# A hybrid attention and SSD layer on one core: where its last projection's weights are loaded and summed, and how far ahead its tiles are fetched

## The chip, the cores and the metric

One core of a Trainium2 chip runs the whole kernel in one launch. The metric is the device time of that launch in microseconds (us), the median of several runs. TensorE (PE) multiplies; VectorE (DVE), ScalarE (ACT) and GpSimd (POOL) do elementwise work; SyncE (SP) only issues transfers. ACT can issue transfers too.

## What is computed

One layer over 1024 positions of width 1024, in float32. The reference, cut to what matters here:

```python
h = rmsnorm(x, pre_norm_mix) * (1.0 + scale_m) + shift_m
q_lat, kv_lat, k_idx, w_idx, z, xbc, dt_raw, g_a, g_b = split(h @ w_in)
y_a = sparse_mla_attention(...) @ w_o_attn
y_b = ssd_mixer(z, xbc, dt_raw, ...) @ w_o_ssd      # begins with a causal convolution of xbc
mix = (sigmoid(g_a) * y_a + sigmoid(g_b) * y_b) @ w_out
x = x + gate_m * rmsnorm(mix, post_norm_mix)
h2 = rmsnorm(x, pre_norm_ffn) * (1.0 + scale_f) + shift_f
u_gate, u_up = split(h2 @ w_ffn_in)                 # 1024 -> 2 x 2816
f = (silu(u_gate) * u_up) @ w_ffn_out               # 2816 -> 1024
x = x + gate_f * rmsnorm(f, post_norm_ffn)
```

## The kernel before

Activations lie transposed: 128 channels on the partitions, 512 positions (one *half*, `b` = 0 or 1) along the free dimension. Every float32 factor is split into a rounded part `hi` and a remainder `lo`, and a product is three matmuls, hi by hi, lo by hi and hi by lo. A weight piece of 128 x 512 is loaded by SP, its `hi` is made by ACT and its `lo` by POOL; an activation's `lo` is mostly made by DVE. So a weight passes through three engines before PE can use it, and its raw buffer is free again when POOL is done.

Instructions are traced in program order. A scheduler (`TC = dict(schedule_with_timeline_sim=True)`) then gives each engine an order of its own; buffers are handed out from rotating sets (`bufs=`), and semaphores follow from the data. An engine works strictly in the order it was given, and SP's queue likewise: an instruction that waits holds up all behind it. The kernel steers this order with edges that cost no semaphore: `in_order` fixes PE's order to the program's, and `behind` puts an instruction after the one that `barrier` holds for its engine. A `Stream` (`W`) loads the weights of most stages (`load`, lines L144 to L153); `next` keeps two pieces ahead of the one in use.

The stages, in the order in which PE works through them:

- Projections. `FILL` gives 44 weight tiles: five groups of four convolution tiles (`conv_group`, `conv`), 16 z tiles, 8 gate tiles. The first are worked on beside the indexer, from 79 us on.
- Attention with its `beside` work: `ada_slow` (L310 on) forms columns of the modulation by 64 multiplications on POOL from buffers tagged `adaw` (two of them). Then the SSD scan.
- `merge(b)` (L1241 on): for each of eight tiles, 48 matmuls `pos` with `w_o_ssd`; then the gates `d_gb`, `d_sga` and the attention output `d_ya` are loaded and combined with the result (L1249 to L1258), and the merged tile is split.
- `mixed(b)`, the matmuls `pot` with `w_out`, then `residual_steps`: row sums, `rstd` (PE, then DVE, then the power `r` on POOL, L265), `rspread` (PE, `prn`, L271), the residual sum, and the same once more for the next norm. `ffn_input` (L1326 on) applies the modulation; for half 0 it makes `h2h` and `h2l`.
- The FFN's first projection uses seven products in place of eight (a Strassen scheme over two halves of channels, positions and inputs). `ffn_sums` makes the sums of activations that it needs. `early` computes two of the products for 18 tiles and fills PE beside half 1's residual: `for n in (2, 1, 9, 2)` says how many of its steps stand before each step of the residual. It writes its results to DRAM, except for the last two tiles, which it keeps (`KEPT`, `held`). `gate_up(t)` does the other five products of a tile, of 12 matmuls each: it loads four weight quarters (`a11`, `a12` from the upper rows, `a21`, `a22` from the lower; tags `w0` with four buffers, `w1` with three), makes sums of them on DVE (L1447, L1448, L1462, L1465; `s1`, `s2` in tag `w2`, three buffers), splits each (`w_parts`, L1389 on ACT, L1390 on POOL), and evicts with DVE (L1454, L1461, L1464, L1467).
- Between the `gate_up` tiles stand 12 `weight_sums` units (L1496 on). Each loads four pieces of `w_ffn_out`, makes four differences of them on POOL (L1502 to L1505), and stores them to `d_t` in DRAM.
- The output projection, seven products again (0 to 6), each with four column tiles `c`, and 33 matmuls for each. `ffn_w` (L1589 on) loads a weight piece through SP from `w_ffn_out` or `d_t` (L1593) and splits it; the split pieces rotate through five `hi` and five `lo` buffers. `prepare` makes the next product's activations during this one's tiles: it loads `al` tiles from `d_a` (L1545; tag EV, nine buffers for everything), sums them on DVE into `S2` and `S3` (L1559 to L1562), and splits. ACT or DVE evicts each column tile. At the end come the last row sums and the output.

Of the kernel before, what the change touches and what calls it, by code (L numbers as in the profile page):

```python
# [67 lines left out]
def build(tc, a, dbg=None, stop=99, slots=None):  # L68
# [56 lines left out]
    def behind(ins):  # L125

        i = ins.ins
        if i.engine in barrier:
            tc.add_manual_dep(i, barrier[i.engine], mybir.DependencyInfo(
                mybir.DependencyClass.NoSync, mybir.DependencyReason.DATA), reason="behind")  # L130


    class Stream:
# [13 lines left out]
        def load(self):  # L147
            src, kt = self.q[len(self.tiles)]
            raw, hi, lo = self.tile(0, F32), self.tile(1, F32R), self.tile(2, F32R)
            behind(SP.dma_start(raw[:, :kt], src))  # L150
            behind(S.activation(hi[:, :kt], raw[:, :kt], AF.Copy))  # L151
            behind(G.tensor_tensor(lo[:, :kt], raw[:, :kt], f(hi[:, :kt]), op=OP.subtract))  # L152
            self.tiles.append((hi, lo))  # L153
# [157 lines left out]
    def ada_slow(j):  # L311
# [3 lines left out]
        for h, t in enumerate(ts):  # L315
            behind(SP.dma_start(t, a["ada_w"][j - 16][:, 4 * h:4 * h + 4]))
            behind(G.tensor_tensor(t, t, cs[:, 4 * h:4 * h + 4, None].to_broadcast([P, 4, P]), op=OP.mult))  # L317
# [617 lines left out]

    def conv_group(g):
        for t in group_tiles(g):
            conv_out(conv(*t))

# [300 lines left out]

    def merge(b, alloc):  # L1241

        MG = []
        for t in range(8):
            W.plan(col_tile(a["w_o_ssd"][t]))
            p = bank_d("pos")
            dense([(p, b, ALL)], wpieces(list(range(16))), YB[b])
            m, ld = EV("mrg"), EV("sgb")
            SP.dma_start(ld, d_gb[t][:, half(b)])  # L1249
            S.activation(ld, ld, AF.Sigmoid)  # L1250
            V.tensor_tensor(m, p, rys[b], op=OP.mult)
            G.tensor_tensor(m, m, ld, op=OP.mult)
            ld, ga = EV("yal"), EV("sgal")
            SP.dma_start(ld, d_ya[t][:, half(b)])
            SP.dma_start(ga, d_sga[t][:, half(b)])
            S.activation(ga, ga, AF.Sigmoid)
            V.tensor_tensor(ld, ld, ga, op=OP.mult)
            V.tensor_tensor(m, m, ld, op=OP.add)  # L1258
            hi, lo = alloc("mg")
            split_to(m, hi, lo)  # L1260
            MG.append(([hi] * 2, [lo] * 2))
        return MG
# [63 lines left out]
    def ffn_input(b, x1):  # L1326

        for t in range(8):
            h2 = x1[t]
            if b == 0:  # L1330
                hi, lo = H_("h2h", dt=F32R), H_("h2l", dt=F32R)
                S.activation(hi, h2, AF.Identity, bias=mod[:, 24 + t:25 + t], scale=am2[:, t:t + 1])
            V.tensor_scalar(h2, h2, am2[:, t:t + 1], mod[:, 24 + t:25 + t], op0=OP.mult, op1=OP.add)
# [47 lines left out]
    def w_load(part, name, t, h):  # L1381
        r = w_tile(part, name)
        i = SP.dma_start(r, a["w_ffn_in"][t][:, 4 * h:4 * h + 4]).ins
        barrier[i.engine] = i.name
        return r
# [23 lines left out]
    held = {}  # L1409

    def early(ts):

        for t in ts:
            w = [w_parts(w_load(0, "a1", t, h)) for h in BS]
# [12 lines left out]
            else:  # L1427
                held[t] = p1, g
            yield

    def gate_up(t):

        a11, a12 = w_load(0, "a11", t, 0), w_load(0, "a12", t, 1)
        a21, a22 = w_load(1, "a21", FT + t, 0), w_load(1, "a22", FT + t, 1)
        if t in held:
            p, (p1, g0) = bank("p0"), held[t]
# [9 lines left out]
        s1, s2 = w_tile(2, "s1"), w_tile(2, "s2")  # L1446
# [32 lines left out]
    with in_order(mybir.EngineType.PE):  # L1479
# [3 lines left out]
        for n in (2, 1, 9, 2):  # L1483
# [7 lines left out]
    KH = FT // 2  # L1491
    KP = (0, 4, 8)
    d_t = dr.tile([4, 4, P, KH, P], F32, name="d_t")
    ws4 = con.tile([P, 4, 4, P], F32, name="ws4", tag="mk")

    def weight_sums(c, k0):  # L1496

        n = min(4, KH - k0)
        b11, b12, b21, b22 = (ws4[:, i, 0:n] for i in range(4))
        for x, t, o in ((b11, c, 0), (b12, 4 + c, 0), (b22, 4 + c, KH), (b21, c, KH)):  # L1500
            behind(SP.dma_start(x, a["w_ffn_out"][t][:, o + k0:o + k0 + n]))
        G.tensor_tensor(b11, b12, b11, op=OP.subtract)  # L1502
        G.tensor_tensor(b12, b22, b12, op=OP.subtract)
        G.tensor_tensor(b22, b22, b11, op=OP.subtract)
        G.tensor_tensor(b21, b22, b21, op=OP.subtract)  # L1505
        for i, x in enumerate((b11, b22, b12, b21)):
            SP.dma_start(d_t[i, c][:, k0:k0 + n], x)

    units = [(c, k0) for c in range(4) for k0 in KP]
# [26 lines left out]
    xs = [[] for _ in range(7)]  # L1536

    def parts(i, src):
        xs[i].append(pair())
        split_to(src, *xs[i][-1])  # L1540

    def raw_a(k, b):

        t = EV("al")
        SP.dma_start(t, d_a[k][:, half(b)])  # L1545
        return t

    def a11(k):
        parts(0, raw_a(k, 0))

    def a12(k):
        parts(1, raw_a(KH + k, 0))

    def a22(k):
        parts(2, raw_a(KH + k, 1))

    def sums(k):
        x21, x22, x11 = raw_a(k, 1), raw_a(KH + k, 1), raw_a(k, 0)
        V.tensor_tensor(S2[k], x21, x22, op=OP.add)  # L1559
# [3 lines left out]

    def sum2(k):
        parts(3, S2[k])

    def sum3(k):
        if k < len(S3):
            x = S3[k]
        else:  # L1570
            x, x21 = raw_a(k, 0), raw_a(k, 1)
            V.tensor_tensor(x, x, x21, op=OP.subtract)
        parts(4, x)

    def sum1(k):
        x = raw_a(k, 0)
        V.tensor_tensor(x, x, S2[k], op=OP.add)
        parts(5, x)

    def sum4(k):  # L1580
        x = raw_a(KH + k, 0)
        V.tensor_tensor(x, x, S2[k], op=OP.subtract)
        parts(6, x)
# [5 lines left out]
    def ffn_w(src, k0, where=None):  # L1589
# [3 lines left out]
        ld = SP.dma_start(raw, src[:, k0:k0 + n]).ins  # L1593
        barrier[ld.engine] = ld.name
# [19 lines left out]
    def squared(src, sacc):  # L1614

        sq = EV("sqm")[:, 0:src.shape[1]]
        S.activation(sq, src, AF.Square)
        if sacc is not None:
            V.tensor_tensor(sq, sq, sacc, op=OP.add)
        return sq  # L1620

    def x1_load(b):

        for t in range(8):
            behind(SP.dma_start(x1s[b][t], d_x1[t][:, half(b)]))
# [10 lines left out]
    wo = a["w_ffn_out"]  # L1636
    sacc = [None, None]
    with in_order(mybir.EngineType.PE):
        for k in range(KH):
            a11(k)  # L1640
        def each(fn, ks=range(KH)):
            return [(fn, k) for k in ks]

        def mixed_up(x, y):
            return [i for two in zip_longest(x, y) for i in two if i]

        ahead = [mixed_up(each(a12), each(sums, range(3))), mixed_up(each(a22), each(sums, range(3, 9))),
                 each(sums, range(9, KH)) + each(sum2), each(sum3), each(sum1), each(sum4), []]

        def prepare(i, c):  # L1650
            todo = ahead[i]
            for fn, k in todo[len(todo) * c // 4:len(todo) * (c + 1) // 4]:
                fn(k)

        srcs = ([wo[c] for c in range(4)], [wo[c][:, KH:FT] for c in range(4)], [d_t[3, c] for c in range(4)],
                [d_t[1, c] for c in range(4)], [d_t[2, c] for c in range(4)], [d_t[0, c] for c in range(4)],
                [wo[4 + c][:, KH:FT] for c in range(4)])

        def product(i, p, c, start):
            prepare(i, c)  # L1660
            for _ in whole(p, [ffn_w(srcs[i][c], k0) for k0 in KP], xs[i], ALL, start):
                pass

        def banks(alloc):
            return [(bank_d if i < alloc else bank)("pfo") for i in range(4)]

        X = banks(0)
        for c in range(4):
            product(0, X[c], c, True)
            S.activation(p1s[c], X[c], AF.Copy)  # L1670
        for c in range(4):
            product(1, X[c], c, False)
            S.activation(fv[0][c], X[c], AF.Copy)
            sacc[0] = squared(X[c], sacc[0])
        X = banks(3)
        for c in range(4):
            product(2, X[c], c, True)
            S.activation(p4s[c], X[c], AF.Copy)
        X = banks(0)
        for c in range(4):  # L1680
            product(3, X[c], c, True)
            V.tensor_tensor(u2s[c], X[c], p1s[c], op=OP.add)
        for c in range(4):
            product(4, X[c], c, False)
            V.tensor_tensor(u3s[c], X[c], p1s[c], op=OP.add)
            V.tensor_tensor(p4s[c], u3s[c], p4s[c], op=OP.subtract)
            sacc[1] = squared(p4s[c], sacc[1])
        X = banks(3)
        for c in range(4):
            product(5, X[c], c, True)  # L1690
            V.tensor_tensor(p1s[c], X[c], u3s[c], op=OP.add)
            sacc[1] = squared(p1s[c], sacc[1])
        x1_load(1)
        for c in range(2):
            product(6, X[c], c, False)
            V.tensor_tensor(u2s[c], X[c], u2s[c], op=OP.add)
# [3 lines left out]
            else:  # L1700
                outputs(1, 0, 512, r, False, False)
        ws = [[ffn_w(srcs[6][c], k0, pair()) for k0 in KP] for c in (2, 3)]
        x1_load(0)
        sums_of = {}
        for sl in (slice(0, 256), slice(256, 512)):
            sq = sacc[0][:, sl]
            for c in (2, 3):
                p = X[c][:, sl]
# [85 lines left out]
```

## Time and profile before

| | |
|---|---|
| median of 3 runs | 2418.3 us (2414.1 to 2419.4) |
| the profiled execution | 2417.7 us, of which its span 2415.9 |
| PE at work | 2334.8 us, 97% of the span |
| DVE / ACT / POOL at work | 1530.8 / 1234.6 / 1164.9 us |
| moved by DMA | 385.05 MB, mean 159 GB/s |
| transfers issued from ACT's queue | 720 packets of 237315 |

The columns of the windows view are: the window and its length in us, then for PE, PEld (weight loads), DVE, ACT and POOL the busy time with the count of instructions, then the granted TensorE clock as a share of full speed, the busy share of the DMA engines and GB/s. In the waits view a row says who waited, on which line, for whom: the sum in us, the number of waits, the longest. In a timeline a row has its start, its duration, the engine (a q stands for its queue of transfers), line, operation, output and inputs, and in brackets the idle time before it and what ended that. In a view of one tile's instructions three durations are the least, the median and the most, in ns.

### The profile page before, as it was taken

How to read it: one execution, taken by the hardware profiler on the slowest of the kernel's cores; microseconds unless marked ns; L12 is line 12 of the kernel's file. 1: busy time of each engine (PE TensorE's matmuls, PEld its weight loads, DVE VectorE, ACT ScalarE, POOL GpSimd, SP SyncE). 2: the span in 40 equal slices, each digit the busy share in tenths (PEclk: the TensorE clock that was granted, in tenths of full speed). 3: DMA queues.
4: the chain of work that ended last, by engine and by line, in shares of the span. 5: the costliest groups of instructions: out<-in, count | busy, mean ns of one | idle time of the engine just before them, and what ended most of it. 6: DMA issues, size and time to landing. Idle time of an engine off the chain costs nothing.

```text
span 2415.9 us, 34903 instructions
## 1 busy us (share of the span) xinstructions
PE 2334.8 (97%) x11808; PEld 1914.8 (79%) x11808; DVE 1530.8 (63%) x2961; ACT 1234.6 (51%) x2376; POOL 1164.9 (48%) x915
## 2 busy tenths in 40 slices
PE   7999999999999999999999999999999999999997
PEld 5788888888887888887877877878777887888786
DVE  4566776499656666666678774445376665638565
ACT  4446665567445555556676654534454222345432
POOL 2721112322234455443445546556577677765645
PEclk9999999999999999999999999999999999999998
DMA  7223212522212222324678775654464676558455
GB/s 273 92 88 128 70 62 79 165 93 92 101 57 92 98 97 79 103 96 138 224 246 277 227 249 198 217 181 165 159 220 138 210 248 237 190 182 307 149 178 170
DMA packets 237315, 385.05 MB, mean 159 GB/s; under 512 B 23968, under 2 KB 91728, under 8 KB 237136
## 3 DMA queue, kind: packets, MB, share of 16 engines
q1 hardware_dynamic: 236416, 382.24, 47.5%
q8 instruction: 93, 1.52, 0.3%
q14 instruction: 86, 0.70, 0.1%
q10 hardware_dynamic: 720, 0.58, 0.1%
HBM read 288.07 MB, written 97.80 MB: 160 GB/s over the span
## 4 chain that ended last, share of the span: by engine, by line
PE 47%; DVE 7%; POOL 5%; DMA 5%; issue 4%; ACT 3%; SPq 1%; POOLq 0%; DVEq 0%; ACTq 0%
PE p L1396 9%; PE pw L236 7%; PE pos L226 6%; PE pfo L1610 4%; PE plg L780 4%; PE pot L226 3%; PE po L829 2%; PE pt L813 2%; PE poa L236 2%; POOL wr L1390 2%; PE puq L226 2%; DMA ws<-w_ffn_out 1%; DMA al<-d_a 1%; PE pyd L1077 1%; PE pst L1082 1%
## 5 line engine op out<-in xcount | busy, mean ns | idle before, releaser
L152 POOL TENSOR_TENSOR wlo<-wraw,whi 128x512 fp32r<-128x512 f32 x246 | 344.2, 1402 | 524.3 <-ACT whi L151 461.9
L1396 PE MATMUL p<-xh,wr 128*128 128x512 f32 x880 | 276.1, 392 | 9.4 <-DVE u L1461 5.1
L151 ACT ACTIVATE whi<-wraw 128x512 fp32r<-128x512 f32 x246 | 153.5, 626 | 196.6 <-issue 45.2
L1396 PEld LDWEIGHTS p<-xh,wr 128*128 128x128 f32 x880 | 166.5, 189 | 46.7 <-DVE u L1461 6.0
L1390 POOL TENSOR_TENSOR wr<-a,wr 128x512 fp32r<-128x512 f32 x110 | 153.9, 1413 | 55.9 <-ACT wr L1389 47.7
L1396 PE MATMUL p<-xl,wr 128*128 128x512 f32 x440 | 172.2, 391 | 0.0
L247 POOL TENSOR_TENSOR fwl<-fw,fwh 128x512 fp32r<-128x512 f32 (+1 forms) x78 | 112.0, 1441 | 107.1 <-ACT fwh L246 100.8
L792 ACT ACTIVATE lg<-lg,mx 128x256 f32<-128x256 f32 (+7 forms) x128 | 99.0, 773 | 71.0 <-DVE mx L789 70.0
L317 POOL TENSOR_TENSOR adaw<-adaw,cs 128x512 f32<-128x512 f32 x64 | 66.7, 1043 | 128.2 <-DMA adaw<-ada_w 113.4
L1389 ACT ACTIVATE wr<-a 128x512 fp32r<-128x512 f32 x110 | 68.0, 628 | 114.3 <-PE p L1396 92.1
L1396 PE MATMUL p<-h2h,wr 128*128 128x512 f32 x352 | 111.7, 394 | 0.0
L640 ACT ACTIVATE junk<-acc,cand__2203 128x1024 bf16<-128x1024 f32 (+2 forms) x96 | 86.2, 898 | 45.8 <-DVE cand__2203 L683 29.9
L226 PE MATMUL pos<-yh,wlo 128*128 128x512 f32 x256 | 101.0, 395 | 3.9 <-POOL wlo L152 3.8
L591 DVE SCALAR_TENSOR_TENSOR acc<-rel,widx,acc 128x384 f32<-128x384 f32 (+2 forms) x90 | 87.1, 987 | 24.9 <-ACT rel L586 24.7
L586 ACT ACTIVATE rel<-prel 128x512 f32<-128x512 f32 (+3 forms) x160 | 77.1, 523 | 48.6 <-PE prel L585 45.0
L226 PE MATMUL pos<-yh,whi 128*128 128x512 f32 x256 | 100.8, 394 | 0.3 <-ACT whi L151 0.3
L226 PE MATMUL pos<-yw,whi 128*128 128x512 f32 x256 | 100.4, 392 | 0.0
L1396 PEld LDWEIGHTS p<-xl,wr 128*128 128x128 f32 x440 | 83.2, 189 | 17.2
L638 DVE TENSOR_SCALAR_CACHE_REDUCE junk<-acc,cand__2212 128x896 bf16<-128x896 f32 (+2 forms) x96 | 88.5, 922 | 1.5
L813 PE MATMUL pt<-ident,lg 128*128 128x128 f32 x576 | 84.2, 275 | 5.0 <-ACT lg L792 4.5
L789 DVE CUSTOM_DVE_ANT_0 lg<-plg,nm 128x256 f32<-128x256 f32 (+1 forms) x128 | 51.5, 403 | 58.4 <-PE plg L780 57.7
L818 ACT ACTIVATE pc<-pt 128x512 f32<-128x512 f32 (+1 forms) x104 | 58.1, 562 | 52.6 <-PE pt L813 51.4
(657 smaller groups left out, 7286.9 us busy)
## 6 DMA issues: line engine op xcount, KB each, us to landing
wraw<-w_in SPq DMA_DIRECT2D x129, 256.0 KB, 2.7
a<-w_ffn_in SPq DMA_DIRECT2D x124, 256.0 KB, 3.3
al<-d_a SPq DMA_DIRECT2D x92, 256.0 KB, 4.7
adaw<-ada_w SPq DMA_DIRECT2D x64, 256.0 KB, 2.9
al<-d_ac SPq DMA_DIRECT2D x32, 512.0 KB, 5.9
wraw<-w_o_ssd SPq DMA_DIRECT2D x64, 256.0 KB, 3.4
d_a<-g SPq DMA_DIRECT2D x40, 256.0 KB, 3.1
ada<-ada_p SPq DMA_DIRECT2D x16, 512.0 KB, 6.2
```

Source lines behind the costliest of these rows:

```text
L151: behind(S.activation(hi[:, :kt], raw[:, :kt], AF.Copy))
L152: behind(G.tensor_tensor(lo[:, :kt], raw[:, :kt], f(hi[:, :kt]), op=OP.subtract))
L226: T.matmul(o, wt[:, k0 + i, :], xs[k][xi][b][:, sl], start=pi == 0 and i == 0 and wt is hi and xi == 0, stop=pi == len(pcs) - 1 and i == l ...
L236: T.matmul(o, wt[:, k0 + j, :], xs[k][xi][b], start=i == 0, stop=i == 23)
L247: (lo_eng or V).tensor_tensor(lo, src, f(hi), op=OP.subtract)
L638: V.tensor_scalar(jk, y, a_, 0.0, op0=op, op1=OP.add, accum_out=o)
L780: T.matmul(p[:, 0:w2], st[qi], KVT[ki][:, o_:o_ + w2], start=x == 0, stop=x == 2)
L792: S.activation(lg[:, 0:n], lg[:, 0:n], AF.Exp, scale=-1.0, bias=m, accum_out=rr[:, 2 * t + hh:2 * t + hh + 1])
L813: T.transpose(ptv[:, hh, t, :], PR[hh, t][:, j * P:(j + 1) * P], ident)
L1390: G.tensor_tensor(w[:, 1], src, f(w[:, 0]), op=OP.subtract)
L1396: T.matmul(p, w[:, wi, i], X[x][i][xi], start=start and i == 0 and k == 0, stop=i == 3 and k == 2, skip_group_check=True)
L1610: T.matmul(p, w[wi][:, k - k0], xs[k][xi][:, sl], start=start and k == 0 and i == 0, stop=k == KH - 1 and i == 2, skip_group_check=True)
```

## The change

1. **Weight sums.** The 12 `weight_sums` units move from between the `gate_up` tiles to behind the last 12 convolution tiles (groups 2 to 4). Their buffers are now the two `adaw` tiles and the two halves of attention's `vt` tile; their loads stand behind the last weight load issued on SP. `ada_slow`'s loads move behind the weight load that is current at the fourth z tile.
2. **Merge.** The three loads and both sigmoids, and the product of two of them, stand before the tile's matmuls. `ffn_input`'s instructions on ACT and DVE go behind the last merged tile's split, and `barrier` on SP becomes the last of the merge's loads.
3. **`early` and `gate_up`.** The lower weights of the two kept tiles are loaded during `early`, and their upper weights are kept (one pair in the `vt` tile). Lower weights rotate through five buffers (`w1` and `adaw`), the sums through five (`w2`, `uh`, `ul`). The list becomes (2, 1, 9, 3). These loads no longer move `barrier`.
4. **Output projection.** Weight pieces are loaded by ACT's queue (`S.dma_start`). Activations are loaded one step (one column tile) before the step that works on them. Some of the sums move: 0 and 1 into product 0, four of them share the loads of product 1, the rest stand in product 2. The first instruction of most preparations is chained behind the last eviction on its engine (`mark`, `held_to`). `x1_load(0)` moves ahead of the last weights.

The diff, cut to its core:

```diff
     def conv_group(g):
         for t in group_tiles(g):
             conv_out(conv(*t))
+            if g > 1:
+                weight_sums(*next(units))
...
         elif kind == "z":
             t = next(n_z)
             gate(1 + t, d_z[t], AF.Silu)
+            if t == 3:
+                ada_after = [W.issue]
...
         for t in range(8):
             W.plan(col_tile(a["w_o_ssd"][t]))
+            sb, ld, ga = EV("sgb"), EV("yal"), EV("sgal")
+            for x, src in ((sb, d_gb), (ld, d_ya), (ga, d_sga)):
+                i0 = SP.dma_start(x, src[t][:, half(b)]).ins
+            S.activation(sb, sb, AF.Sigmoid)
+            S.activation(ga, ga, AF.Sigmoid)
+            V.tensor_tensor(ld, ld, ga, op=OP.mult)
             p = bank_d("pos")
             dense([(p, b, ALL)], wpieces(list(range(16))), YB[b])
...
+    LOWER = [("w1", n_slots["hi"])] * 3 + [("adaw", 2)] * 2
+    SUMS = [("w2", n_slots["lo"])] * 3 + [("uh", 1), ("ul", 1)]
...
+            if t == EARLY - KEPT - 1:
+                low_w = [lower(EARLY - KEPT + i) for i in range(KEPT)]
...
-        for n in (2, 1, 9, 2):
+        for n in (2, 1, 9, 3):
...
-    for n, t in enumerate([*range(EARLY - KEPT, EARLY), *range(EARLY - KEPT), *range(EARLY, FT)]):
+    for t in [*range(EARLY - KEPT, EARLY), *range(EARLY - KEPT), *range(EARLY, FT)]:
         gate_up(t)
-        for u in units[12 * max(0, n - 4) // 18:12 * max(0, n - 3) // 18]:
-            weight_sums(*u)
...
         raw = w_tile(0, "fw")[:, 0:n]
-        ld = SP.dma_start(raw, src[:, k0:k0 + n]).ins
-        barrier[ld.engine] = ld.name
+        S.dma_start(raw, src[:, k0:k0 + n])
...
+    def held_to(ins):
+        i = ins.ins
+        if i.engine in last:
+            tc.add_manual_dep(i, last[i.engine], mybir.DependencyInfo(
+                mybir.DependencyClass.NoSync, mybir.DependencyReason.DATA), reason="behind")
...
+        def step(i, c):
+
+            n = 4 * i + c
+            loaded.append([load() for load, _ in tasks[n + 1]])
+            for (_, work), x in zip(tasks[n], loaded[n]):
+                work(x)
+            return [ffn_w(srcs[i][c], k0) for k0 in KP] if n < 26 else None
```

More of the change, by code (lines that the diff above doesn't have):

```diff
@@ L149, in load @@
             raw, hi, lo = self.tile(0, F32), self.tile(1, F32R), self.tile(2, F32R)
-            behind(SP.dma_start(raw[:, :kt], src))
+            self.issue = behind(SP.dma_start(raw[:, :kt], src))
             behind(S.activation(hi[:, :kt], raw[:, :kt], AF.Copy))
@@ L934, in group_tiles, with weight_sums @@
         return (16 + g, d_bc[g, 0]), (24 + g, d_bc[g, 1]), (2 * g, d_xs[2 * g]), (2 * g + 1, d_xs[2 * g + 1])
+    KH = FT // 2
+    d_t = dr.tile([4, 4, P, KH, P], F32, name="d_t")
+    units = iter([(c, k0) for c in range(4) for k0 in (0, 4, 8)])
+    sum_bufs = [wp.tile([P, 4, P], F32, name="adaw", tag="adaw", bufs=2) for _ in range(2)]
+    both = vp.tile([P, NT, P], F32, name="vt", bufs=1)
+    sum_bufs += [both[:, 0:4], both[:, 4:8]]
+    def weight_sums(c, k0):
+        n = min(4, KH - k0)
+        b11, b12, b21, b22 = (x[:, 0:n] for x in sum_bufs)
+        for x, t, o in ((b11, c, 0), (b12, 4 + c, 0), (b22, 4 + c, KH), (b21, c, KH)):
+            tc.add_manual_dep(SP.dma_start(x, a["w_ffn_out"][t][:, o + k0:o + k0 + n]).ins, W.issue, mybir.DependencyInfo(
+                mybir.DependencyClass.NoSync, mybir.DependencyReason.DATA), reason="behind")
+        G.tensor_tensor(b11, b12, b11, op=OP.subtract)
+        G.tensor_tensor(b12, b22, b12, op=OP.subtract)
+        G.tensor_tensor(b22, b22, b11, op=OP.subtract)
+        G.tensor_tensor(b21, b22, b21, op=OP.subtract)
+        for i, x in enumerate((b11, b22, b12, b21)):
+            SP.dma_start(d_t[i, c][:, k0:k0 + n], x)
     def conv_group(g):
@@ L1536, in build, with mark, raw_a, parts @@
     xs = [[] for _ in range(7)]
[L1538 to L1559, printed above, removed]
+    last = {}
+    def mark(ins):
+        last[ins.ins.engine] = ins.ins.name
+    def held_to(ins):
+        i = ins.ins
+        if i.engine in last:
+            tc.add_manual_dep(i, last[i.engine], mybir.DependencyInfo(
+                mybir.DependencyClass.NoSync, mybir.DependencyReason.DATA), reason="behind")
+    def raw_a(*which):
+        ts = [EV("al") for _ in which]
+        for t, (k, b) in zip(ts, which):
+            SP.dma_start(t, d_a[k][:, half(b)])
+        return ts
+    def parts(i, src, anchored=False):
+        hi, lo = pair()
+        xs[i].append((hi, lo))
+        ins = S.activation(hi, src, AF.Copy)
+        if anchored:
+            held_to(ins)
+        V.tensor_tensor(lo, src, f(hi), op=OP.subtract)
+    def plain(i, k0, b):
+        return [(lambda k=k: raw_a((k0 + k, b)), lambda x: parts(i, x[0], True)) for k in range(KH)]
+    def sum_of(k, x21, x22, x11):
+        held_to(V.tensor_tensor(S2[k], x21, x22, op=OP.add))
         V.tensor_tensor(S2[k], S2[k], x11, op=OP.subtract)
@@ L1624, in x1_load @@
         for t in range(8):
-            behind(SP.dma_start(x1s[b][t], d_x1[t][:, half(b)]))
+            SP.dma_start(x1s[b][t], d_x1[t][:, half(b)])
     def outputs(b, c0, cn, r, share, end):
@@ L1636, in build @@
     wo = a["w_ffn_out"]
+    low, high = [wo[c] for c in range(4)], [wo[c][:, KH:FT] for c in range(8)]
     sacc = [None, None]
     with in_order(mybir.EngineType.PE):
[L1639 to L1662, printed above, removed]
@@ L1679, in build @@
[L1679 to L1685, printed above, removed]
+        for k in ks:
+            parts(0, raw_a((k, 0))[0])
+        loaded = [[load() for load, _ in tasks[0]]]
+        srcs = low, high[0:4], d_t[3], d_t[1], d_t[2], d_t[0], high[4:8]
+        def step(i, c):
[4 more added lines that the diff above has]
+            return [ffn_w(srcs[i][c], k0) for k0 in KP] if n < 26 else None
@@ new lines, in products, with four @@
+        def products(i, alloc=None):
+            for c in range(4):
+                ws = step(i, c)
+                for _ in whole(banks[c], ws, xs[i], ALL, alloc is not None):
+                    pass
+                yield c, banks[c]
+        def four(alloc):
+            return [(bank_d if i < alloc else bank)("pfo") for i in range(4)]
+        banks = four(0)
+        for c, p in products(0, 0):
+            mark(S.activation(p1s[c], p, AF.Copy))
+        for c, p in products(1):
+            S.activation(fv[0][c], p, AF.Copy)
+            sacc[0] = squared(p, sacc[0])
@@ L1686, in build @@
+        banks = four(3)
+        for c, p in products(2, 3):
+            mark(S.activation(p4s[c], p, AF.Copy))
+        banks = four(0)
+        for c, p in products(3, 0):
+            mark(V.tensor_tensor(u2s[c], p, p1s[c], op=OP.add))
+        for c, p in products(4):
+            V.tensor_tensor(u3s[c], p, p1s[c], op=OP.add)
             V.tensor_tensor(p4s[c], u3s[c], p4s[c], op=OP.subtract)
             sacc[1] = squared(p4s[c], sacc[1])
[L1688 to L1691, printed above, removed]
+        banks = four(3)
@@ L1692, in build @@
+        for c, p in products(5, 3):
+            V.tensor_tensor(p1s[c], p, u3s[c], op=OP.add)
             sacc[1] = squared(p1s[c], sacc[1])
@@ L1694, in build @@
         for c in range(2):
-            product(6, X[c], c, False)
-            V.tensor_tensor(u2s[c], X[c], u2s[c], op=OP.add)
+            for _ in whole(banks[c], step(6, c), xs[6], ALL, False):
+                pass
+            V.tensor_tensor(u2s[c], banks[c], u2s[c], op=OP.add)
             sacc[0] = squared(u2s[c], sacc[0])
```

144 lines of the change are left out of this document (77 added, 67 removed).

## The prediction

> **What bounds the kernel now.** I read the page first, then the span cut into windows, then what TensorE (PE) waited for in the short windows, then single engines' timelines there.
>
> ```profile
> span 2415.9 us, 34903 instructions
> PE 2334.8 (97%) x11808; PEld 1914.8 (79%) x11808; DVE 1530.8 (63%) x2961; ACT 1234.6 (51%) x2376; POOL 1164.9 (48%) x915
> ```
>
> PE is the bound: 81 us of idle time in 2416. The change takes no matmul away, so it can only fill gaps, and only gaps in the stages that it touches. Since matmuls overlap in the records, I count them instead of trusting the busy column. The next rows are windows: length, busy time and count of PE, PEld, DVE, ACT, POOL, then granted clock, DMA share, GB/s.
>
> ```profile
> 240.00:300.00 60.00, 60.00 (x282) 50.41 (x281) 44.73 (x69) 37.77 (x74) 10.59 (x8) 1.00 0.20 70
> 1600.00:1620.00 20.00, 16.82 (x71) 13.54 (x70) 14.34 (x22) 8.70 (x16) 15.56 (x7) 0.94 0.35 114
> 1680.00:1700.00 20.00, 17.26 (x73) 13.10 (x72) 17.14 (x17) 10.15 (x17) 14.71 (x10) 1.00 0.35 116
> 1760.00:1780.00 20.00, 16.85 (x77) 13.71 (x76) 10.19 (x13) 9.82 (x18) 17.72 (x14) 0.95 0.89 284
> 1780.00:1800.00 20.00, 20.00 (x86) 16.50 (x86) 19.97 (x26) 7.26 (x13) 9.03 (x6) 0.97 0.48 159
> 1840.00:1860.00 20.00, 16.62 (x61) 12.87 (x60) 9.94 (x15) 5.76 (x11) 10.06 (x8) 0.83 0.31 107
> 1900.00:1920.00 20.00, 18.56 (x82) 15.02 (x82) 13.54 (x15) 5.58 (x9) 17.25 (x13) 1.00 0.69 249
> 2000.00:2020.00 20.00, 18.51 (x82) 15.03 (x81) 12.00 (x14) 5.06 (x9) 13.86 (x11) 1.00 0.54 181
> 2020.00:2040.00 20.00, 18.24 (x81) 14.81 (x80) 12.94 (x17) 4.94 (x8) 14.34 (x10) 1.00 0.71 245
> 2040.00:2060.00 20.00, 18.64 (x82) 15.08 (x81) 10.78 (x16) 4.84 (x8) 16.31 (x12) 1.00 0.70 245
> 2240.00:2260.00 20.00, 17.08 (x67) 13.12 (x66) 14.37 (x22) 9.20 (x18) 15.09 (x7) 0.91 0.58 190
> 2360.00:2380.00 20.00, 16.17 (x58) 11.98 (x57) 10.02 (x14) 9.14 (x17) 13.99 (x12) 0.83 0.63 196
> 2100.00:2160.00 60.00, 60.00 (x266) 49.71 (x265) 22.59 (x29) 24.04 (x43) 45.60 (x35) 1.00 0.45 151
> 2175.00:2375.00 200.00, 192.51 (x831) 156.68 (x830) 134.20 (x154) 93.01 (x169) 109.17 (x76) 0.98 0.64 208
> ```
>
> The row from 2100 is a full one: 266 matmuls of 512 columns in 60 us, 0.2256 us each, 88.7 in 20 us. What a 20 us row lacks of 88.7, times 0.2256, is what that window loses, slow clock included: 3.5 us from 1680, 6.2 us from 1840, 6.3 us in the four rows from 1900 and 2000 to 2060 (6.7, 6.7, 7.7 and 6.7 matmuls), 11.8 us in the two from 2240 and 2360 (21.7 and 30.7). The row from 1760 holds small matmuls too, so there I take its idle time, 3.15 us, and up to 1.6 us for the clock (0.95 and 0.97 over two rows). The row from 1600 loses 4.0 us. PE's waits name what came last in each:
>
> ```profile
> PE pos L226 <- POOL wlo L152: 3.2, 1, 3.2
> PE pot L1270 <- POOL wlo L152: 2.4, 2, 1.5
> PE prn L271 <- POOL r L265: 3.2, 1, 3.2
> PE p L1396 <- DVE u L1461: 3.4, 1, 3.4
> PE p L1396 <- DVE u L1464: 4.3, 3, 1.5
> PE p L1396 <- DVE u L1461: 1.8, 1, 1.8
> PE pfo L1610 <- POOL fwl L247: 2.2, 1, 2.2
> PE pfo L1610 <- DVE al L247: 1.9, 5, 0.7
> ```
>
> **The change part by part.** I add what each part fills, against the profiled execution's own 2417.7 us (its span of 2415.9 and 1.8 around it), which lies 0.6 us under the median of the runs, 2418.3.
>
> *End of the second merge* (window 1680; loss 3.5 us). DVE's timeline there:
>
> ```profile
> 1693.76 1.66 DVE L1335 TENSOR_TENSOR h2l<-xr,h2h 128x512 fp32r<-128x512 f32 x1
> 1695.34 1.75 DVE L1257 TENSOR_TENSOR yal<-yal,sgal 128x512 f32<-128x512 f32 x1
> 1697.19 0.69 DVE L1258 TENSOR_TENSOR mrg<-mrg,yal 128x512 f32<-128x512 f32 x1
> ```
>
> The last merge tile's gating (L1257, L1258) stands behind `ffn_input` of the other half (L1335), and the w_out splits on POOL stand between its other half of L1335. The change loads the gates before the matmuls, so that L1257 is done early, and chains `ffn_input` on ACT and DVE behind the last merge split. That half is needed only when `early` starts, after eight tiles of 24 matmuls, 43 us, and it is twelve instructions on DVE, at most 20 us at the 1.66 of the row. It also holds three EV buffers through a tile's matmuls; with nine that leaves room for two tiles. I take 2.5 of 3.5; the ends are 3.5, and 0 if the splits stay late.
>
> *One more `early` step before the second row spread* (window 1760). PE waits 3.15 us for `r`; the list (2, 1, 9, 3) puts 12 more matmuls, 2.7 us, into that wait, and part of the clock comes back. The chain behind it (x1 times the spread, the FFN sums) starts no earlier. I take 3.0; the ends are 0 (POOL takes the added step's split before `r`) and 4.75.
>
> *First two `gate_up` tiles* (window 1840, 6.2 us). DVE again:
>
> ```profile
> 1851.47 0.69 DVE L1447 TENSOR_TENSOR s<-a,a 128x512 f32<-128x512 f32 x1 [4.54 <-DMA a<-w_ffn_in]
> 1852.27 0.69 DVE L1448 TENSOR_TENSOR s<-s,a 128x512 f32<-128x512 f32 x1
> 1852.88 0.68 DVE L1462 TENSOR_TENSOR a<-a,a 128x512 f32<-128x512 f32 x1
> 1853.48 0.68 DVE L1461 TENSOR_TENSOR u<-p,p 128x512 f32<-128x512 f32 x1
> ```
>
> The eviction L1461 that PE waits for is ready, but behind the next tile's weight sum L1447 in DVE's order, and that waits 4.54 us for a load whose buffer (three of them) came free late. The change keeps the upper weights of the two kept tiles, loads their lower ones during `early`, and gives lower weights and sums five buffers each. I take 5.5 of 6.2; what could be late next is the FFN sums, and only the fifth product needs the last of them.
>
> *The other `gate_up` tiles* (6.3 us) lose by the same chain, lengthened by the weights' sums between its steps on SP and POOL:
>
> ```profile
> L1501 SPq DMA_DIRECT2D ws<-w_ffn_out x48: 376/430/932, 1890.1 to 2132.6; - x48
> L1502 POOL TENSOR_TENSOR ws<-ws x12: 1232/1318/1812, 1896.0 to 2135.2; 128x512 f32<-128x512 f32 x8, 128x384 f32<-128x384 f32 x4
> L1507 SPq DMA_DIRECT2D d_t<-ws x48: 319/323/384, 1897.7 to 2145.1; - x48
> ```
>
> Both go: 12 units of four subtractions (about 5.3 us of POOL at 1.32 each), four loads (0.43) and four stores (0.32), 3.0 us of SP's issuing. I take 5.0 of 6.3.
>
> *The same units behind the last twelve convolution tiles.* All 96 transfers and 48 subtractions arrive there, and the loads wait in SP's queue for the last W load, the stores for POOL. Queued behind them are the next tile's W loads and the convolutions' stores; PE waits for the W pieces. The row from 240 is that stage: PE full, eight POOL splits in 60 us, two a tile, so four tiles at most and a unit every 15 us. POOL would go from 10.6 to 32 of 60 us, SP gains 12 us, DMA from 70 GB/s to about 210 (32 tiles of 128 x 512 x 4 bytes more in 60 us). PE has two W pieces in hand, 48 matmuls or 10.8 us, longer than a unit's 5.3 us of POOL. I take 0.5 us; the ends are 0 and 24 (2 us for each unit). The adaw tiles are lent to the sums and come back long before attention reads them; the vt tile must be free when attention starts.
>
> *The output stage* (2175 to 2375; 11.8 us lost). Weight loads leave SP for ACT's queue, activations are loaded one step ahead, and preparation is chained behind the evictions:
>
> ```profile
> SPq L1593 <- POOL fwl L247: 99.6, 53, 8.1
> 2246.52 12.41 POOL L247 TENSOR_TENSOR fwl<-fw,fwh 128x512 fp32r<-128x512 f32 x4 [3.54 <-ACT fwh L246]
> 2246.98 11.05 SPq L1593 DMA_DIRECT2D fw<-d_t  x4
> L246 ACT ACTIVATE fwh<-fw 128x512 fp32r<-128x512 f32 x48 | 30.0, 624 | 30.3 <-PE pfo L1610 19.2 <-POOL fwl L247 9.9 <-DMA fw<-d_t 0.8
> L247 POOL TENSOR_TENSOR fwl<-fw,fwh 128x512 fp32r<-128x512 f32 x48 | 77.3, 1614 | 59.0 <-ACT fwh L246 55.8 <-DMA fw<-d_t 3.1
> 2410.95 1.60 ACTq L1634 DMA_DIRECT2D out<-aq  x3
> ```
>
> SP stood 99.6 us at weight loads whose buffer POOL had not yet split, up to 8.1 us at a time, with the activation loads (`al`) behind them. Freed of that, `al` comes earlier and the waits on DVE's `al` go. But now ACT stands there. It is busy 93.0 of 200 us; 84 issues (seven products, four column tiles, three pieces) at SP's 0.32 add 27, or 45 at the 0.53 of the last row, which leaves 62 to 80 us for waits. Each weight has nine pieces of lead (four raw buffers, five split ones) of eleven matmuls on average, 22 us of PE. I take 6.0 of 11.8; the ends are 11.8, and the loss of the second rival below. The window from 1600 I leave as it is: its `wlo` is late beside the residual's sums, which nothing here touches.
>
> Sum: 2.5 + 3.0 + 5.5 + 5.0 + 6.0 = 22.0 gained, less 0.5 for the units and 1.0 for order that shifts elsewhere (a quarter of the 4.0 us that one unlucky order costs in the window from 1600): 2417.7 - 20.5 = 2397.2.
>
> **The rivals.** *The ScalarE queue brings nothing.* The output stage keeps its 11.8 us, because POOL's splits set the weights' pace whoever issues: 2397.2 + 6.0 = 2403. For it: PE's longest single wait there is on POOL's `fwl`. Against: SP's 99.6 us with `al` behind it. The Trainium skill says as much in "DMA: Bandwidth & Descriptors", section "Issuing engines are not separate DMA queues": issuing from several engines saves only the sequencer's time. The trace shows more at stake than that, namely the wait in front of the issue.
>
> *ACT becomes the bound (slower).* If ACT's order is strictly split, wait for POOL, issue, then each of 84 pieces costs 0.62 + 1.61 + 0.32 = 2.55 us, 214 us, and ACT's other work in the stage (93.0 less 84 x 0.62 = 52) 41 more: 255 us against 200, 55 us longer. With 16.0 - 1.5 gained before, that is 2417.7 - 14.5 + 55 = 2458. It decides from 14.5 us of ACT standing that reaches PE: a quarter of it already ends above the old time. For it: the 12.41 us that four POOL splits took would hold ACT, and evictions behind it. Against: ACT has other work to do while POOL splits, and 22 us of lead.
>
> *The units starve the convolutions.* 2 us of PE for each of twelve: 2397.2 + 23.5 = 2421. Against: PE is full with POOL at a sixth.
>
> *All the losses go:* 3.5 + 4.75 + 6.2 + 6.3 + 11.8 = 32.6 us, 2385.
>
> **How the numbers follow.** The forecast, 2397, has a chance of 0.58 and its own range of 2389 to 2402; no gain from the queue 0.18; ACT the bound 0.11; starved convolutions 0.07; everything filled 0.06. The range from 2385 to 2414 holds the forecast, the first rival and half-way mixtures, and leaves out about 0.18. A measurement can tell 0.2% here, 4.8 us. Faster by more than that: the first, second and last case and a little less, 0.80; slower 0.12 (ACT, and a starved stage at its dear end); the same 0.08.
>
> **What would show it.** Right: the waits of L1396 on L1461 and L1464 all but gone, no sums on POOL after 1860; the sums between 200 and 420 with PE still full at 1.00; the wait for `r` under 1 us; SP's waits on `fwl` gone and ACT standing for POOL, without PE waiting for evictions. Wrong: PE under 60.00 in the convolutions; in the output stage, waits of PE on ACT (`ah`, `fwh`) or on banks not evicted; or the 1840 gap still there with another releaser.

## The result and the profile after

The changed kernel takes 2399.4 us (median of 4 runs, 2393.3 to 2402.3) against 2418.45 for the kernel before, with a fourth run beside the three above: a ratio of 0.9922, 95% interval 0.9897 to 0.9946. The forecast was 2397. The profiled execution took 2397.2, its span 2395.4.

The page's first lines, for the changed kernel:

```profile
span 2395.4 us, 34903 instructions
PE 2327.0 (97%) x11808; PEld 1911.8 (80%) x11808; DVE 1551.6 (65%) x2961; ACT 1232.8 (51%) x2376; POOL 1167.7 (49%) x915
```

The matmuls are as many as before (11808). PE's idle time fell from 81 to 68 us, and its busy time by 7.8 us; one thing that goes into the latter is the granted clock, which was 0.91 and 0.83 in the rows from 2240 and 2360 before, and is 1.00 in all rows below but one. These are windows at about the same places of the work as those shown of before (columns as there):

```profile
240.00:300.00 60.00, 60.00 (x283) 50.37 (x282) 49.32 (x67) 36.98 (x71) 36.86 (x25) 1.00 0.57 198
1680.00:1700.00 20.00, 20.00 (x90) 16.57 (x89) 9.21 (x11) 9.07 (x15) 14.01 (x11) 1.00 0.41 132
1776.00:1796.00 20.00, 18.41 (x84) 14.98 (x83) 16.77 (x24) 9.26 (x17) 13.01 (x11) 1.00 0.75 239
1836.00:1856.00 20.00, 14.48 (x56) 10.90 (x54) 10.16 (x12) 8.64 (x17) 14.91 (x12) 0.91 0.29 93
1995.00:2015.00 20.00, 20.00 (x90) 16.58 (x89) 13.86 (x18) 5.97 (x10) 9.13 (x8) 1.00 0.40 128
2035.00:2055.00 20.00, 20.00 (x90) 16.58 (x89) 12.00 (x15) 5.58 (x9) 10.22 (x8) 1.00 0.44 142
2233.00:2253.00 20.00, 20.00 (x90) 16.58 (x89) 17.91 (x22) 9.98 (x19) 9.80 (x7) 1.00 0.82 271
2168.00:2368.00 200.00, 198.79 (x897) 164.90 (x897) 130.08 (x161) 95.19 (x172) 111.21 (x83) 1.00 0.68 217
```

Read the counts against 88.7, as the forecast did. The second merge's end, the later `gate_up` tiles and the output stage (897 matmuls in 200 us where 831 stood) are full or nearly so. So are the convolutions, as before, though POOL works 36.9 of 60 us there and DMA moves 198 GB/s instead of 70. In the window from 1776 PE still waits for `r`. One has stayed as it was: 56 matmuls from 1836, where the first `gate_up` tiles lie; before it held 61. PE's waits of the changed kernel, line, tile and engine waited for, then sum, times and longest:

```profile
PE prn L272 <- POOL r L266: 5.6, 6, 1.6
PE p L1432 <- DVE u L1526: 3.1, 1, 3.1
PE pos L227 <- POOL wlo L153: 2.7, 5, 0.7
PE p L1432 <- DVE g L1519: 2.5, 1, 2.5
PE pos L227 <- ACT whi L152: 2.0, 2, 1.3
PE p L1432 <- POOL wr L1426: 0.9, 1, 0.9
```

No wait of `pfo` is left. L1526 is what was L1461 (`u`), and its 3.1 us stand in the place of the 3.4 before.

### The profile page after: what moved, and what is told of

Same layout as the page of the kernel before. It is cut to its first block, busy times and chain, and to the rows that moved or that the text cites. A ratio compares the mean times of both kernels' runs of the same rounds, so it can differ in the third digit from the quotient of the medians.

```text
span 2395.4 us, 34903 instructions
## 1 busy us (share of the span) xinstructions
PE 2327.0 (97%) x11808; PEld 1911.8 (80%) x11808; DVE 1551.6 (65%) x2961; ACT 1232.8 (51%) x2376; POOL 1167.7 (49%) x915
## 5 line engine op out<-in xcount | busy, mean ns | idle before, releaser
L1426 POOL TENSOR_TENSOR wr<-a,wr 128x512 fp32r<-128x512 f32 x107 | 149.0, 1404 | 115.0 <-ACT wr L1425 77.9
L248 POOL TENSOR_TENSOR fwl<-fw,fwh 128x512 fp32r<-128x512 f32 (+1 forms) x78 | 106.7, 1378 | 104.9 <-ACT fwh L247 70.0
L593 DVE SCALAR_TENSOR_TENSOR acc<-rel,widx,acc 128x384 f32<-128x384 f32 (+2 forms) x90 | 102.1, 1158 | 16.4 <-ACT rel L588 16.1
L1426 POOL TENSOR_TENSOR wr<-s,wr 128x512 fp32r<-128x512 f32 x44 | 62.2, 1416 | 51.2 <-ACT wr L1425 43.0
```

What stands on the lines that cost most here:

```text
L248: (lo_eng or V).tensor_tensor(lo, src, f(hi), op=OP.subtract)
L593: V.scalar_tensor_tensor(acc[i][:, 0:n], rel[:, 0:n], ws, acc[i][:, 0:n], op0=OP.mult, op1=OP.add)
L1426: G.tensor_tensor(w[:, 1], src, f(w[:, 0]), op=OP.subtract)
```

## The experiments

In each, the time is compared with runs of the kernel before on the same chip. Where a stage is given, it is read from a profiled execution, from the first matmul of the stage to the last.

**Each part alone.** Four kernels are the kernel before with one of the four parts of the change, as the change makes it; but part 3 leaves the list of `early` steps as it was, and its loads still move `barrier`, because the units of weight sums, which stay between the `gate_up` tiles there, are ordered by it.

> The kernel before with part 1 of the change alone: the twelve weight_sums units behind the convolution tiles, ada_slow's loads moved, nothing else. The forecast's terms (D: 5.0 gained in the other gate_up tiles; 0.5 lost in the convolutions) give 2414. My theory after reading the changed kernel's trace, in which the first convolution matmul stood 9.2 us later and the end of attention 1.5 us later than before: the units cost about as much ahead of the merges as they gain behind, gate_up 5 shorter, everything up to attention 2 to 5 longer, 2415 to 2418. Rival: the 9.2 us at the start belong to another order of instructions that this part does not bring alone; then the start is as before and the time is 2412 to 2414.

Measured: 0.9980 (0.9966 to 0.9993), some 5 us faster. `gate_up` ran from 1834.1 to 2161.6, 327.5 us, against 335.5 before:

```profile
L1396 PE MATMUL p<-xh,wr x880: 387/389/794, 1839.0 to 2174.6; 128*128 128x512 f32 x176
```

```profile
L1423 PE MATMUL p<-xh,wr x880: 387/389/628, 1834.1 to 2161.6; 128*128 128x512 f32 x176
```

The first row is the kernel before, the second the one with part 1. My theory had the gain eaten up ahead of the merges, and that fell: the merge began at 1455.3 (before 1456.0). The first convolution matmul did stand late, at 87.8; why, is told below.

> The kernel before with part 2 alone: the merge's loads and sigmoids ahead of its matmuls, ffn_input chained behind the last merged tile. The forecast's term A gives 2.5 gained, 2415.8. My theory from the changed kernel's trace (first merge 4.0 us longer, second 1.7 shorter): the second merge's end is gained, but the three loads ahead of the matmuls put the first merge's weights back, so about 2 us lost, 2420. Rival: the first merge's loss came from attention's end or from another part; then this one is 1 to 3 us faster, 2415 to 2417.

Measured: 1.0000 (0.9985 to 1.0015). Both theories were half right. The stretch at the merge's end (first row: before, second: with part 2) does its 196 matmuls in 44 us instead of 48:

```profile
1686.00:1734.00 48.00, 45.26 (x196) 36.22 (x195) 18.19 (x19) 20.62 (x37) 29.25 (x23) 1.00 0.36 117
```

```profile
1683.00:1727.00 44.00, 44.00 (x196) 36.43 (x195) 22.25 (x21) 24.05 (x41) 31.25 (x22) 1.00 0.33 107
```

But from the first `pos` matmul to the last, with half 0's `pot` matmuls between the two merges, PE takes 228.9 us on average in six profiles without this part (227.2 to 230.5) and 231.4 in eight with it (228.9 to 233.6). The ranges overlap; on average more than half of the 4 us is given back there. The waits of `pos` for `wlo` and `whi` do not say why: they come to 2.0 us on average without this part and to 2.3 with it. What is new in each of the eight profiles, and in none of the six, is a wait of 0.7 to 1.6 us early in the first merge: the row spread (`prn`) waits for `r`. In the kernel with part 2 (PE's wait, then DVE ahead of it):

```profile
PE prn L271 <- POOL r L265: 1.5, 1, 1.5
```

```profile
1466.49 0.69 DVE L1259 TENSOR_TENSOR yal<-yal,sgal 128x512 f32<-128x512 f32 x1 [2.22 <-ACT sgal L1258]
1467.10 0.15 DVE L263 TENSOR_SCALAR v<-p 128x4 f32<-128x4 f32 x1
```

The product that the part moves ahead of the matmuls (L1259) waits for ACT's sigmoid, and behind it in DVE's order stands `v`, from which POOL makes `r`. So it is in all eight, and in none of the six does that product stand ahead of `v`. This is about half of the 2.5 us; where the rest goes is not shown.

> The kernel before with part 3 alone, its list of early steps left at (2, 1, 9, 2): lower and kept weights loaded ahead, longer rotations for lower weights and sums; the units of weight sums stay between the gate_up tiles. The forecast's term C (5.5 of 6.2 us at the first two gate_up tiles) gives 2413. My theory: that gap does not close, because in the changed kernel's trace 6.5 us of waits of the same matmuls on the same two additions stood there again, so the start of gate_up gains 0 to 1; the longer rotations take 1 to 3 us off the other tiles: 2415 to 2418. Rival: the gap closes here, and it was another part that opened a new one: 2412 to 2414.

Measured: 1.0031 (1.0016 to 1.0045), slower; neither theory went so far. Its waits from 1840 to 2180:

```profile
PE p L1396 <- DVE u L1491: 9.8, 5, 5.2
PE p L1396 <- DVE g L1484: 1.4, 1, 1.4
PE p L1396 <- DVE u L1494: 1.0, 2, 0.5
```

The wait for `u` that this part was to remove has grown from 3.4 to 5.2 and stands before more tiles; `gate_up` took 340.7 us.

> The kernel before with part 4 alone: the whole new output stage, with its weights on ScalarE's queue, activations one step ahead and the preparation chained behind evictions. The forecast's term E (6.0 gained) gives 2412; its first rival (the queue brings nothing) gives 2418, its second (ScalarE becomes the bound) up to 2472. My theory from the changed kernel's trace, where this stage was 13.3 us shorter: the whole loss of 11.8 us goes and the tail is 1 to 3 us shorter: 2404 to 2407. Rival: half of the 13.3 needs the other parts; then 2410 to 2413.

Measured: 0.9956 (0.9944 to 0.9969), 10.6 us, as the theory had it in kind and nearly in size. The stage is as full as in the changed kernel without any of the other parts.

**Why part 3 costs time.** DVE in the changed kernel at the gap (start, duration, idle time before it and what ended that):

```profile
1841.92 0.81 DVE L1512 TENSOR_TENSOR s<-a,a 128x512 f32<-128x512 f32 x1 [4.04 <-DMA a<-w_ffn_in]
...
1848.01 0.68 DVE L1519 TENSOR_TENSOR g<-p,p 128x512 f32<-128x512 f32 x1
1853.12 0.69 DVE L1512 TENSOR_TENSOR s<-a,a 128x512 f32<-128x512 f32 x1 [4.44 <-DMA a<-w_ffn_in]
1853.91 0.69 DVE L1513 TENSOR_TENSOR s<-s,a 128x512 f32<-128x512 f32 x1
1854.52 1.75 DVE L1527 TENSOR_TENSOR a<-a,a 128x512 f32<-128x512 f32 x1
1856.19 0.68 DVE L1526 TENSOR_TENSOR u<-p,p 128x512 f32<-128x512 f32 x1
```

It is the picture of before: an eviction (L1519, L1526) behind a sum (L1512) that waits for its load. By DVE's order of instructions these two sums belong to the third and the fourth `gate_up` tile; without part 3, and so with rotations of three, the sums at the same two places are those of the second and third. (In the changed kernel the second tile's sum already stands at 1808.0.) So the scheduler spends two more buffers on taking the sums of one tile further ahead, and the load is again the one that is not there. Three kernels test that.

> The changed kernel without part 3: rotations of three for lower weights and sums, nothing kept or loaded ahead for the first gate_up tiles; the list (2, 1, 9, 3) stays. By the forecast's term C the first gate_up tiles lose 5.5 us more than in the changed kernel: 2405. My theory now, from part 3 alone being 0.3% slower: part 3 lets DVE's order take the sum of one tile more ahead, so that the same two evictions stand behind a sum whose load is still a tile later; without it gate_up takes 327 to 328 us instead of 330.4, and the whole 2395 to 2398. Rival: part 3 cost time only because the units of weight sums shared SP's queue with its loads; without the units it is neutral or better: 2399 to 2403.

Measured: 2391.7 us, 0.9910 (0.9895 to 0.9924). `gate_up` lasts 327.5 us as with part 1 alone.

> The changed kernel with one thing added: on DVE, without a semaphore, the first sum (s1) of the third and fourth gate_up tiles is ordered behind the last eviction (the addition to g1 after the fourth product) of the first. If the order is the cause, the 6.5 us of waits at the first two tiles (0.9, 2.5 and 3.1) fall to under 1.5 and gate_up from 330.4 to about 325; 2393 to 2395. If the load itself is late whatever DVE does (the sum is then missing when PE needs it), the wait moves to the third or fourth tile and gate_up stays at 329 to 331: 2398 to 2400.

```diff
+        sums_behind(V.tensor_tensor(s1, a21, a22, op=OP.add))
...
+        done[order_n[0]] = V.tensor_tensor(g1, p5, g1, op=OP.add).ins.name
```

Here `sums_behind` adds, for the third and the fourth tile, a `NoSync` edge from `done` of the first. Measured: 2388.4 us, 0.9895 (0.9878 to 0.9913).

> The changed kernel without part 3 and with the same ordering, here for the third gate_up tile alone: its first sum behind the last eviction of the first tile. If the order is the cause and part 3's buffers are not needed, the one wait of 3.4 us that the kernel with part 1 alone had there goes, gate_up takes 324 to 325 us, and this is the fastest: 2392 to 2395. If with three buffers the third tile's load then comes too late, the wait moves to the third tile and it equals the kernel without part 3: 2395 to 2398.

Measured: 2384.0 us, 0.9876 (0.9860 to 0.9891). The `gate_up` rows of the changed kernel, of the one without part 3, of the one with the ordering, and of the one with both:

```profile
L1432 PE MATMUL p<-xh,wr x880: 389/389/795, 1837.0 to 2167.4; 128*128 128x512 f32 x176
```

```profile
L1433 PE MATMUL p<-xh,wr x880: 389/389/794, 1833.0 to 2160.5; 128*128 128x512 f32 x176
```

```profile
L1432 PE MATMUL p<-xh,wr x880: 387/389/504, 1834.2 to 2158.8; 128*128 128x512 f32 x176
```

```profile
L1433 PE MATMUL p<-xh,wr x880: 389/389/504, 1827.9 to 2150.5; 128*128 128x512 f32 x176
```

330.4, 327.5, 324.6 and 322.6 us. With the ordering alone the waits on DVE in these tiles fall from 5.6 to 1.3 us; with both, PE waits once, for POOL:

```profile
PE p L1433 <- POOL wr L1427: 0.6, 1, 0.6
```

The order was the cause of the gap, shown from both sides: leave the buffers and order two sums, and the gap closes; take the buffers away as well, and it stays closed and nothing else is lost. It is not all that part 3 costs: with the order right, `gate_up` still takes 2.0 us more with the part (324.6, one profile) than without it (322.6, and 322.5 in the last kernel below), and what makes these 2 us is not shown.

**What filled the output stage.** Part 4 holds a queue, loads one step ahead, sums moved from product to product, and an order.

> The changed kernel with the output stage's 84 weight loads issued by SP again, all else as in the changed kernel (activations a step ahead, preparation behind evictions). Forecast's working: SP's waits for POOL's split come back in front of the activation loads, so most of the stage's gain goes: 2404 to 2410. The forecast's first rival: the queue brings nothing, 2398 to 2401. Between: loads a step ahead have most of the gain already, 2400 to 2403.

```diff
-        S.dma_start(raw, src[:, k0:k0 + n])
+        SP.dma_start(raw, src[:, k0:k0 + n])
```

Measured: 2393.6 us, 0.9918 (0.9903 to 0.9933), the changed kernel's own ratio. SP stands for POOL's split again, and PE does not notice: its row of the output stage and SP's longest waits in it.

```profile
2162.00:2362.00 200.00, 200.00 (x893) 165.91 (x893) 139.67 (x163) 98.42 (x177) 110.94 (x80) 1.00 0.68 221
```

```profile
SPq L1677 <- POOL fwl L248: 78.6, 52, 4.3
```

> The kernel before with one line of part 4: the output stage's weight loads issued by ScalarE, no longer by SP. The forecast's working (SP's 99.6 us of waits stood in front of the activation loads) gives half of the 6.0 at least: 2410 to 2415, against its first rival (POOL sets the pace, whoever issues): as before. My theory now, since the changed kernel with SP's queue is as fast as with ScalarE's: the queue alone brings nothing, within 0.1% of before; first to last matmul of the output stage 239 to 245 us as in the other runs with the old stage.

```diff
-        ld = SP.dma_start(raw, src[:, k0:k0 + n]).ins
-        barrier[ld.engine] = ld.name
+        S.dma_start(raw, src[:, k0:k0 + n])
```

Measured: 2417.8 us, 1.0017 (1.0002 to 1.0031): not a gain, rather a small loss, and the stage took 247.3 us to the end of the span. PE waits there for DVE's `al` and now for ACT as well:

```profile
PE pfo L1609 <- DVE al L247: 4.3, 5, 2.1
PE pfo L1609 <- ACT fwh L246: 2.4, 1, 2.4
```

> The changed kernel without the chaining of the output stage's preparation behind evictions (held_to orders nothing); the activations are still loaded one step ahead and the weights are on ScalarE's queue. If the loads a step ahead are what filled the stage, its matmuls stay gapless (29.92 and 89.76 us for products 2 and 3 to 5) and the time is the changed kernel's, 2396 to 2400. If the order on DVE and ScalarE is what filled it, as at gate_up, gaps of 0.4 to 2 us behind DVE's al come back, 3 to 10 us in all: 2402 to 2409.

Measured: 2401.1 us, 0.9953 (0.9937 to 0.9970). Both theories had a part. Products 2 to 5 stay gapless to 0.2 us, so the loads a step ahead or the moved sums fill the middle, or both; no run has one without the other. Without the order the last part, from product 6 to the end, takes 54.3 us instead of 49.2; the row sums' matmul waits there, first in this kernel, then in the changed one:

```profile
PE p L261 <- DVE sqm L1702: 5.5, 3, 3.3
PE pfo L1693 <- POOL fwl L248: 0.6, 1, 0.6
```

```profile
PE p L261 <- DVE sqm L1702: 2.2, 2, 2.0
```

**The list, and the fastest version.**

> The kernel before with the list (2, 1, 9, 3) in place of (2, 1, 9, 2), nothing else. The forecast's term B gives 3.0 gained (ends 0 and 4.75): about 0.12% faster, and the wait for r near 1780 from 3.15 to under 1. My reading of the other traces: 1 to 3 us in the stage from the first early matmul to the first of gate_up (104 to 107 us without the longer list, 101.5 to 103.1 with it), the wait for r near 1.6. Rival: the step added here is missing behind the residual, and the first gate_up tile is late by as much: no gain.

Measured: 2406.9 us, 0.9974 (0.9957 to 0.9991). The stage from the first `early` matmul to the first of `gate_up` took 100.9 us, and from 1735 to 1840 PE waits once, and not for `r`; the rival fell:

```profile
PE p L1396 <- POOL wr L1390: 0.5, 1, 0.5
```

> The fastest so far (the changed kernel without part 3, the third gate_up tile's first sum ordered behind the first tile's last eviction, 2384.0 us) with the output weights on SP's queue again. If the queue matters nowhere, the same within 0.1%; from the two traces with the new stage (last part 47.4 us with SP, 49.2 with ScalarE) 1 to 2 us faster, 2382 to 2384. If ScalarE's queue is of use once PE comes sooner to the stage, 2 to 5 us slower.

Measured: 2380.2 us, 0.9872 (0.9852 to 0.9893), not to be told from 0.9876. The fastest version is thus the change without its part 3, with one sum ordered by hand, and either queue.

## Why the forecast came out right, and which steps did not

The total was right by luck, because errors cancelled: C was off by 8.8 us, and D and E by 3.0 and 4.0 the other way. The terms, in us, each as a mean over the profiles with and without the part (counts in brackets; a row leaves out kernels that hold its part only by half, and the rows of `gate_up` those with a sum ordered by hand):

| term | forecast | without | with | measured |
|---|---|---|---|---|
| units in the convolutions (first `pos` matmul) | +0.5 | 1454.7 (6) | 1455.6 (8) | +0.9 |
| A: merges, first `pos` to last | part of A | 228.9 (6) | 231.4 (8) | +2.5 |
| A: last `pos` to first `early` matmul | -2.5 | 47.7 (6) | 43.75 (8) | -3.9 |
| B: `early` to `gate_up` | -3.0 | 105.6 (6) | 101.9 (8) | -3.8 |
| D: `gate_up`, units gone, three buffers | -5.0 | 335.5 (5) | 327.5 (2) | -8.0 |
| C: `gate_up`, part 3 on top of that | -5.5 | 327.5 (2) | 330.8 (3) | +3.3 |
| E: output stage to the end | -6.0 | 241.1 (5) | 231.1 (5) | -10.0 |
| order that shifts elsewhere | +1.0 | | | in the rows above |

Measured, they add to -19.0, as the ratio has it (0.78% of 2418.45 is 18.9; its interval goes from 13 to 25). The 0.9 of the first row cannot be told from nothing: the six profiles without the units lie between 1451.3 and 1459.0.

**C failed.** The forecast said of the first two tiles that the sum "waits 4.54 us for a load whose buffer (three of them) came free late", and took 5.5 of 6.2 for two more buffers and earlier loads. The reading of the row was right, the conclusion not: the eviction was late because of its place in DVE's order, and that order is made anew by the scheduler, which used the buffers to run further ahead. The signs that the forecast named showed it: the 1840 gap still there, though with the same releasers.

**A** had the gap right and left out a price. The forecast saw that three EV buffers are held through a tile's matmuls, and charged nothing for the merges themselves, where three loads and two sigmoids now come ahead of a tile's matmuls. They lost 2.5 us of the 3.9 gained, about half of it because a product that was moved ahead now stands on DVE in front of the work for `r`, and waits there for a sigmoid.

**D and E were mis-sized.** For D the four windows were not all of the stage's loss: 8.0 us went where 6.3 were counted. For E the forecast took half of the two windows' 11.8 us; 10.0 us went on average, and products 1 to 5 have no gap left (29.92 us each). The later window is the last part's: from product 6 to the end it was 55 to 57 us in the profiles of the old stage and is 48 to 49 in the new. The earlier one was in good part an accident of the one profiled execution: in the kernel with the longer list the instructions of the output stage stand in the same order on every engine, its `pfo` never waits for `fwl`, and the stage takes 239.4 us instead of 244.7. With part 1, 2 or 3 alone `pfo` does not wait for `fwl` either, and the stage takes 239.3 to 241.4.

**The first rival** said that the queue brings nothing, and therefore that the stage keeps its loss. Its premise is right, by two kernels (0.9918 with SP's queue against 0.9922; 1.0017 for the queue alone); the conclusion isn't, since the gain came from the loads ahead (with the moved sums) and from the order. Nor is its reason: POOL works as long in the stage as before (111.2 of 200 us, before 109.2), and PE is full. "DMA: Bandwidth & Descriptors" in the Trainium skill, section "Issuing engines are not separate DMA queues", says that issuing from several engines saves only the time on the sequencer, and here the trace agrees: 0.33 us for each of 84 issues, and no time gained. The forecast's objection, SP's 99.6 us of waits with `al` behind them, fell: with 78.6 us of such waits PE is full in the kernel that asks for `al` a step earlier.

**The second rival** did not come. ACT works 95.2 of 200 us in the window of the output stage and stands 16.5 us for POOL's splits (14.4 before), but PE waits for no eviction. (A quarter of this rival's 55 us is 13.8, just under the 14.5 gained elsewhere, so the forecast's remark that a quarter already ends above the old time is off by a little.) **Starved convolutions** did not come either: in the window from 240 PE is at 60.00 and the clock at 1.00 with the sums beside it. **B** came a little larger than taken; the wait for `r` fell to 1.6 us, where under 1 was forecast, and with the list alone there was none.

**The start is not later with part 1.** The first convolution matmul stands at 79.2 to 85.1 us in six profiles with the old order of the front (mean 81.9) and at 84.6 to 90.6 in eight with the new one (86.7). But PE has more to do ahead of it, as the counts of PE's matmuls up to that point show, in the kernel before and in the changed one:

```profile
0.00:79.25 79.25, 61.27 (x344) 44.86 (x345) 41.37 (x79) 31.98 (x55) 32.02 (x28) 0.94 0.62 224
0.00:88.46 88.46, 68.04 (x365) 50.68 (x366) 41.17 (x80) 35.77 (x61) 29.79 (x26) 0.88 0.53 192
```

Part 1 changes the order there, and 21 matmuls for other results (`pp`, `pmi`) come first; at 0.2256 us each they are 4.7 of the 4.8 us. PE's 345th matmul stands at 81.9 us on average in both groups. So the order of these matmuls changed, and the front is no slower for it.

## What to carry to other kernels

Where an engine's order is made by a scheduler, a wait for a buffer may be a wait for a place in that order: give more buffers, and the instruction that is not ready is only another one. Before counting a gap as gained, name the instruction that stands ahead of the late one, and pin that pair with an edge that costs nothing; here it took 5 to 6 us off `gate_up`, where the rotations had added 3. And a queue that waits long for its turn need not be a loss: here SP's 78.6 us of waits cost PE nothing once what stands behind them was asked for a step earlier.

## What the runs showed besides

Identical instructions vary from one execution to the next by as much as a part of this change is worth. In the kernels with part 2, 3 or 4 alone, the queue alone and the list alone, every engine has up to attention the order of the kernel before, and so the same 344 matmuls come first, yet their first convolution matmuls stand at 85.0, 85.1, 79.2, 79.9 and 82.7 us, and before at 79.3. The kernel before and the one with part 2:

```profile
L226 PE MATMUL pw<-h0h,whi x88: 388/389/504, 79.3 to 669.8; 128*128 128x512 f32 x88
```

```profile
L226 PE MATMUL pw<-h0h,whi x88: 388/389/504, 85.0 to 673.1; 128*128 128x512 f32 x88
```

So a gap of one profile is a sample. The 3.2 us wait for `wlo` near 1600, which the forecast called an unlucky order, is another case: with the list alone the order up to there is the same, and the longest such wait of `pos` is 0.6 us.

With the weight sums on POOL beside the indexer, DVE's accumulations there take 17% longer (before, then the changed kernel; busy us, mean ns, then idle time):

```profile
L591 DVE SCALAR_TENSOR_TENSOR acc<-rel,widx,acc 128x384 f32<-128x384 f32 (+2 forms) x90 | 87.1, 987 | 24.9 <-ACT rel L586 24.7
```

```profile
L593 DVE SCALAR_TENSOR_TENSOR acc<-rel,widx,acc 128x384 f32<-128x384 f32 (+2 forms) x90 | 102.1, 1158 | 16.4 <-ACT rel L588 16.1
```

The mean is 985 to 987 ns in the six profiles without the sums there, and 1137 to 1187 in the eight with them. The Trainium skill says in "SBUF — State Buffer", section "SBUF: two separate sides", that DVE and GpSimd share one pair of ports, and that a DVE instruction with two inputs in SBUF and a GpSimd instruction that reads SBUF block each other there: whoever starts first has the pair for its whole instruction. The longer means agree with that, though no run here isolates it. It costs 15 us of DVE; PE stays full in the window from 240, and DVE's idle time before those instructions falls from 24.9 to 16.4 us.
